# Half of a sparse weighted row sum taken from TensorE to VectorE, and the sparse work put in another order

## The chip, the cores and the metric

The kernel runs on one core of one Trainium2 chip. The metric is the device time of one execution in microseconds (us); lower is better. The median of three runs of the kernel before is 1426.06 us (1424.3 to 1428.26).

## The reference, cut to what matters

One layer on 512 tokens of width 1024, in float32. A token mixer and a LayerNorm come first, then PEER, a retrieval among 16384 experts, and a second LayerNorm. Only PEER matters for the change:

```
scores -> top 16 x 16 candidates -> expert_idx, gates     (8 heads x 16 = 128 experts per token)
u   = u_tab[expert_idx]                                   (128 rows of 1024 per token)
act = gelu(sum_d x[d] * u[k, d]) * gates[k]
out = sum_k act[k] * v_tab[expert_idx[k]]
x   = LayerNorm(alpha * x + out)
```

## The kernel before, in words

The kernel computes PEER in two ways at once. For the last 256 tokens it is dense: a main loop goes over the 128 blocks of 128 experts, loads a block of both tables (512 KB each) on SyncE's queue, and multiplies on TensorE, with the routing written out as a matrix `ring` that holds each token's gate for each expert. For the first 256 tokens, two groups of 128, it is sparse: GpSimd gathers single rows of the tables by indirect DMA, 128 rows (512 KB) to a gather, into nine buffers `gat` (`NGAT`, line 59).

**The sparse work.** It has two parts for each group i. The u part: gather j fetches, for each of the 128 tokens (one a partition), the row of its expert in slot j, by column j of `idxs[i]`. VectorE multiplies it with the token's x and sums up, which gives column j of `dots` (`sparse_u`, line 1042). When 128 columns are there, `sparse_act` makes `coef` of them (Gelu, times the gate), and `sparse_turn` transposes it on TensorE to `coefT`. The v part: gather t fetches all 128 experts' rows of one token, by column t of `idxT`, one expert a partition. `sparse_v` takes four such tiles, for the tokens r, 32 + r, 64 + r and 96 + r, and multiplies each on TensorE by a 128x32 piece of `expand`, a matrix of zeros with one column of coefficients, so that each token's sum lands in its own row of the two PSUM banks `facc` (line 1102). After 32 such groups the sums of 128 tokens are complete. `finish_a` then adds alpha times x from `x1s[i]`, and `finish_q`, `finish_s`, `finish_b` and `finish_c` make the LayerNorm.

**The order.** It is written out by hand. `gq` is the queue of gathers and `sparse` the queue of their consumers, in the same order; `pull` (line 1024) issues gathers while fewer than nine buffers are held. In the main loop, iteration b calls `work` four times, which takes consumers from the queue by a quota in units (`QUOTA`, line 63): 5 units an iteration up to iteration 13, 3.5 up to 30, then the rest of 512 spread evenly up to 125. A u counts 1 unit, a v group 4. The queue holds 128 u of group 0, then by turns 4 u of group 1 and one v group of group 0, then the finish of group 0, then the 32 v groups of group 1 and its finish.

**An iteration of the main loop** (line 1267) also has, for the dense part: `u_split` and `v_split`, which split a block into a high and a low part (ScalarE copies, VectorE subtracts, line 118); `h_run`, 24 matmuls for a block's activations (line 1261); `a_mul` and `a_low`, which scale them by the routing (lines 1004 and 118); and `v_tile`, 12 matmuls into PSUM (line 1253). Up to iteration 30 the matmuls with v are in plain float32 (line 1243). In three windows of iterations (`GWIN`, 14 to 30, 38 to 61, 70 to 93) VectorE also builds one-hot matrices (`g_hot`, lines 947 to 957), four instructions in two iterations of three, from which TensorE makes the next part of `ring`.

What must be free for what: each engine takes its instructions in program order. A gather waits for the buffer's last reader, on VectorE for a u and on TensorE for a v. The first v group of group 1 waits until `finish_a` has read the banks of group 0. The finish holds up to three of the nine buffers, for the rows of the norm and as scratch.

Of the kernel before, what the change touches and what calls it, by code (L numbers as in the profile page):

```python
# [10 lines left out]
F32 = mybir.dt.float32  # L11
# [3 lines left out]
I32 = mybir.dt.int32  # L15
U32 = mybir.dt.uint32
AF = mybir.ActivationFunctionType
OP = mybir.AluOpType
# [3 lines left out]
ALPHA = 2.0 ** 0.25  # L22
# [3 lines left out]
D = 1024  # L26
# [16 lines left out]
SPT = 256  # L43
# [58 lines left out]
def hybrid_kernel(ctx, tc, cst, xT, x, w_in, conv_a, vec_a, pool_w, conv_c, w_out, ln,  # L102
                  wq, keysT, uT, u, v, out):
    nc = tc.nc
    act, dve, pe, pool, sp = nc.scalar, nc.vector, nc.tensor, nc.gpsimd, nc.sync
# [8 lines left out]
    def copy_act(o, i, scale=1.0):  # L114
        return act.activation(o, i, AF.Copy, scale=scale)  # L115
# [29 lines left out]
    ident = const.tile([128, 128], F32, name="ident")  # L145
# [11 lines left out]
    x1s = [xtp.tile([128, D], F32, name=f"x1s{i}") for i in range(NU)]  # L157
# [7 lines left out]
    with ExitStack() as fctx:  # L165
# [31 lines left out]
        zero = mx.tile([128, T], BF, name="sp", bufs=1)  # L197
# [442 lines left out]
    mp = ctx.enter_context(tc.tile_pool(name="mp", bufs=1))  # L640
    ring = mp.tile([128, RB, ND], F32, name="ring")
    idxs = [mp.tile([128, 128], I32, name=f"idx{i}") for i in range(NU)]
    gss = [mp.tile([128, 128], F32, name=f"gs{i}") for i in range(NU)]
    idxT = mp.tile([128, SPT], I32, name="idxT")
    expand = mp.tile([128, 4, 31 + 32 * EH], F32, name="expand")
    usplit, uraw, gl = {}, {}, {}

# [42 lines left out]
    def ramp_fill(n):  # L690
        for _ in range(n):
            b, k = divmod(ramp[0], 8)
            if b == (ucount[1] if b < RSPL else RAMP):
                return
            if k == 0:
                ramp[1] = h_psum()
            if b < RSPL:
                h_part(b, ramp[1], [k])
                if k == 7:
                    ramp_split()  # L700
            else:
                u_load(b + 2)
                pe.matmul(ramp[1], uraw[b][:, k, :], native["x"][:, k, :], start=k == 0, stop=k == 7)  # L703
                if k == 7:
                    uraw.pop(b)
                    ucount[1] = b + 1
                    h_gelu(b, ramp[1])
            ramp[0] += 1
# [11 lines left out]
    with ExitStack() as rctx:  # L720
# [176 lines left out]
        def turn(src):  # L897
            ps = fps.tile([128, T], F32, name="b", bufs=6)
            for b in range(SPT // 128, NB):
                pe.transpose(ps[:, 128 * b:128 * b + 128], src[:, b, :], ident)  # L900
            return ps[:, SPT:]
# [12 lines left out]
        ef = rt.tile([128, NU, 128], F32, name="ef")  # L914
# [7 lines left out]
        copy_act(gTh, gf)  # L922
        copy_act(i2T, turn(i2v))
        eps_ = fps.tile([128, T], F32, name="b", bufs=6)
        for i in range(NU):
            pe.transpose(eps_[:, 128 * i:128 * i + 128], ef[:, i, :], ident)
            copy_act(gss[i], gm[:, i, :])
        sub(gTl, gf, gTh)
        ramp_fill(TFILL[3])
        dve.tensor_copy(idxT, eps_[:, :SPT])  # L930

    pctx.close()
    def g_hot(q, tg, where, bufs):
# [83 lines left out]
    gats, gq, sparse = {}, deque(), deque()  # L1017
    held = [0]


    def spare():
        return gp.tile([128, D], F32, name="gat", bufs=NGAT)

    def pull():
        while gq and held[0] < NGAT:
            kind, i, j = gq.popleft()
            t = spare()
            gats[kind, i, j] = t
            held[0] += 1
            if kind == "l":  # L1030
                sp.dma_start(t, ln[2 + i:3 + i, :].to_broadcast([128, D]))
            if kind == "x":
                sp.dma_start(t, x1d[:, NU + i, :])
            if kind not in "uv":
                continue
            table, idx = (u, idxs[i][:, j:j + 1]) if kind == "u" else (v, idxT[:, 128 * i + j:128 * i + j + 1])
            pool.indirect_dma_start(out=t, out_offset=None, in_=table,  # L1037
                                    in_offset=bass.IndirectOffsetOnAxis(ap=idx, axis=0))

    def sparse_u(i, j):  # L1040
        t = gats.pop(("u", i, j))
        dve.scalar_tensor_tensor(t, t, 1.0, x1s[i], op0=OP.mult, op1=OP.mult, accum_out=dots[:, j:j + 1])  # L1042
        held[0] -= 1

    def add_u(i, j):
        gq.append(("u", i, j))
        sparse.append((1, lambda: sparse_u(i, j)))
# [24 lines left out]
    mp2 = ctx.enter_context(tc.tile_pool(name="mp2", bufs=1))  # L1072
    coef = mp2.tile([128, 128], F32, name="coef")
# [4 lines left out]
    facc = [pacc.tile([128, 512], F32, name=f"facc{hf}") for hf in range(2)]  # L1078
# [14 lines left out]
    def sparse_expand(s):  # L1093
        o = 31 + 256 * (s % 2)
        copy_act(expand[:, :, o:o + 32 * 7 + 1:32], coefT[:, :, 8 * s:8 * s + 8])

    def sparse_v(i, r):
        ts = [gats.pop(("v", i, 32 * j + r)) for j in range(4)]
# [7 lines left out]
    fin = {}  # L1106

    def finish_a(key, f, x1):
        fs = mp2.tile([128, 4], F32, name="fs", bufs=4)
        sums, mean, sd = fs[:, 0:2], fs[:, 2:3], fs[:, 3:4]  # L1110
        for hf in range(2):
            cc = slice(512 * hf, 512 * hf + 512)
            dve.scalar_tensor_tensor(x1[:, cc], x1[:, cc], ALPHA, f[hf], op0=OP.mult, op1=OP.add,
                                     accum_out=sums[:, hf:hf + 1])
        dve.tensor_scalar(mean, sums[:, 0:1], sums[:, 1:2], -1.0 / D, op0=OP.add, op1=OP.mult)
        fin[key] = [x1, mean, sd, x1]

    def finish_q(key):
        x1, mean, sd = fin[key][:3]
        if ("s", key, 0) in gats:  # L1120
            junk = gats.pop(("s", key, 0))
            held[0] -= 1
        else:
            junk = spare()
        act.activation(junk, x1, AF.Square, bias=mean, accum_out=sd)
# [26 lines left out]
    def zero(f, *a):  # L1152
        sparse.append((0, lambda: f(*a)))

    def add_v(i, r):
        if r == 0:
            zero(sparse_expand, 1)
        if r in (9, 17):
            zero(sparse_expand, r // 8 + 1)
        for j in range(4):  # L1160
            gq.append(("v", i, 32 * j + r))
        sparse.append((4, lambda: sparse_v(i, r)))

    zero(sparse_act, 0)
    zero(sparse_clear)
    for k in range(34):
        if k < 32:
            for j in range(4):
                add_u(1, 4 * k + j)
        if k == 0:  # L1170
            zero(sparse_turn)
        if k == 1:
            zero(sparse_expand, 0)
        if k == 32:
            zero(sparse_act, 1)
        if k > 1:
            add_v(0, k - 2)
        if k == 32:
            zero(sparse_turn)
    gq.append(("s", 0, 0))  # L1180
    gq.extend(("l", i, 0) for i in range(2))
    zero(finish_a, 0, facc, x1s[0])
    zero(sparse_expand, 0)
    sparse.append((1, lambda: finish_q(0)))
    zero(finish_0)
    sparse.append((1, finish_1))
    for k in range(32):
        add_v(1, k)
    gq.extend(("l", i, 1) for i in range(2))
    gq.extend(("x", i, 0) for i in range(2))  # L1190
    sparse.append((1, lambda: finish_a(128, facc, x1s[1])))
    sparse.append((1, lambda: finish_q(128)))

    quota = []
    for end, n in QUOTA:
        i = end - len(quota)
# [170 lines left out]
```

## Time and profile before

| | |
|---|---|
| median of three runs | 1426.06 us |
| the profiled execution, its own time | 1420.93 us |
| its span | 1419.1 us |
| PE busy | 1322.5 us (93%) |
| DVE busy | 1086.8 us (77%) |
| POOL busy | 779.0 us (55%) |
| ACT busy | 512.5 us (36%) |
| moved by DMA | 439.83 MB, 310 GB/s in the mean |

PE is TensorE's matmuls, DVE VectorE, POOL GpSimd, ACT ScalarE. The shares of busy time are means over stages that differ: the first 410 us or so are the mixer and the routing, and the sparse work fills the rest. They are therefore read by stretches of the span. In a matmul's row the end is modelled, so rows of one line overlap. On VectorE too, an instruction's row can reach some 0.08 us into the next one's; what an instruction costs is the distance between two starts.

### The profile page before, as it was taken

The page shows a single profiled execution, that of the slowest core. Times are in us where ns is not written, and L with a number is a line of the kernel's source. Part 1 is how long each engine was busy: PE and PEld are TensorE (multiplying, and loading weights), DVE is VectorE, ACT ScalarE, POOL GpSimd, SP SyncE. Part 2 cuts the span into 40 slices and gives each one's busy share as a digit, 9 for nine tenths or more (in the row PEclk, how much of TensorE's full clock was granted, in tenths as well). Part 3 has the DMA queues.
Part 4 walks back from the last instruction along what each step waited for, and adds up shares of the span by engine and source line. Part 5 has one row for each costly group of instructions (what it writes and reads, how often), then busy time and mean ns, then how long its engine had stood idle before and what let it go on. Part 6 is the DMA issues. An engine that isn't in the chain of part 4 may idle for free.

```text
span 1419.1 us, 24250 instructions
## 1 busy us (share of the span) xinstructions
PE 1322.5 (93%) x9229; PEld 1006.2 (71%) x9229; DVE 1086.8 (77%) x2292; ACT 512.5 (36%) x735; POOL 779.0 (55%) x687
## 2 busy tenths in 40 slices
PE   9999999989995668998999999999999989999996
PEld 6787889989862234666677777777778767777774
DVE  7876669999987899998788888778888843444445
ACT  4654524321420001323344434334444443333333
POOL 2242317774537786667666665666656545455450
PEclk9999999999998888999999999999999999999998
DMA  6520323223659999999999999999999999999993
GB/s 212 186 63 13 134 84 128 83 75 110 229 199 389 420 411 367 378 375 375 413 377 392 388 385 390 405 419 404 405 403 402 406 364 416 402 419 409 419 408 141
DMA packets 125444, 439.83 MB, mean 310 GB/s; under 512 B 14480, under 2 KB 16528, under 8 KB 125328
## 3 DMA queue, kind: packets, MB, share of 16 engines
q0 software_dynamic: 73728, 268.47, 48.0%
q1 hardware_dynamic: 51312, 168.78, 31.6%
q8 instruction: 72, 1.18, 0.3%
q10 hardware_dynamic: 288, 1.05, 0.2%
q14 instruction: 44, 0.36, 0.1%
HBM read 435.09 MB, written 3.15 MB: 309 GB/s over the span
## 4 chain that ended last, share of the span: by engine, by line
PE 50%; issue 14%; DMA 13%; POOL 11%; DVE 10%; ACT 2%; POOLq 0%; DVEq 0%; SPq 0%; ACTq 0%
PE acc L1253 12%; PE w L1261 11%; POOL gat L1037 10%; DMA gat<-in_v,idxT 8%; PE facc L1102 8%; DMA gat<-in_u,idx 4%; PE b L138 4%; PE b L139 4%; PE b L137 4%; PE w L703 3%; DVE i_top L757 2%; DVE s_top L755 1%; PE z L312 1%; DVE sc L760 1%; DVE gat L1042 1%
## 5 line engine op out<-in xcount | busy, mean ns | idle before, releaser
L1037 POOL DMA_INDIRECT gat<-in_u,idx x256 | 336.5, 1314 | 222.5 <-DVE gat L1042 142.6
L1037 POOL DMA_INDIRECT gat<-in_v,idxT x256 | 280.6, 1096 | 178.6 <-PE facc L1102 100.1
L1042 DVE SCALAR_TENSOR_TENSOR gat<-gat,x1s 128x1024 f32<-128x1024 f32 x256 | 309.4, 1222 | 15.7 <-DMA gat<-in_u,idx 15.1
L1253 PE MATMUL acc<-vh,A 128*128 128x512 f32 x768 | 261.5, 401 | 0.0
L1261 PE MATMUL w<-x1Tdh,whi 128*128 128x256 f32 x832 | 241.7, 291 | 1.6 <-ACT gl L1264 1.4
L1261 PE MATMUL w<-x1Tdl,whi 128*128 128x256 f32 x832 | 235.2, 283 | 0.0
L1261 PE MATMUL w<-x1Tdh,wlo 128*128 128x256 f32 x832 | 234.9, 282 | 0.0
L118 DVE TENSOR_TENSOR vl<-vraw,vh 128x1024 fp32r<-128x1024 f32 x96 | 117.5, 1224 | 121.2 <-ACT vh L115 121.1
L1253 PEld LDWEIGHTS acc<-vh,A 128*128 128x128 f32 x768 | 145.1, 189 | 81.5 <-issue 28.5
L1243 PE MATMUL acc<-vraw,af 128*128 128x512 f32 x248 | 136.9, 697 | 48.6 <-DVE af L1004 45.2
L115 ACT ACTIVATE whi<-wraw 128x1024 fp32r<-128x1024 f32 (+1 forms) x146 | 151.0, 1036 | 48.6 <-DMA wraw<-in_wq 25.5
L1102 PE MATMUL facc<-gat,expand 128*32 128x512 f32 x1024 | 152.5, 600 | 14.8 <-DMA gat<-in_v,idxT 14.1
L1261 PEld LDWEIGHTS w<-x1Tdh,whi 128*128 128x128 f32 x832 | 159.4, 192 | 6.1 <-ACT gl L1264 2.3
L1261 PEld LDWEIGHTS w<-x1Tdl,whi 128*128 128x128 f32 x832 | 159.3, 191 | 2.4
L1261 PEld LDWEIGHTS w<-x1Tdh,wlo 128*128 128x128 f32 x832 | 159.0, 191 | 0.0
L118 DVE TENSOR_TENSOR wlo<-wraw,whi 128x1024 fp32r<-128x1024 f32 (+1 forms) x109 | 131.7, 1210 | 34.7 <-ACT whi L115 34.0
L115 ACT ACTIVATE vh<-vraw 128x1024 fp32r<-128x1024 f32 x96 | 101.4, 1056 | 143.5 <-issue 118.1
L1253 PE MATMUL acc<-vl,A 128*128 128x512 f32 x384 | 151.0, 393 | 0.0
L118 POOL TENSOR_TENSOR wlo<-wraw,whi 128x1024 fp32r<-128x1024 f32 x37 | 92.5, 2504 | 96.0 <-ACT whi L115 96.0
L1243 PEld LDWEIGHTS acc<-vraw,af 128*128 128x128 f32 x248 | 51.1, 219 | 112.3 <-DVE af L1004 61.2
L115 ACT ACTIVATE ring<-w 128x384 f32<-128x384 f32 (+2 forms) x80 | 52.4, 740 | 169.4 <-PE w L973 169.4
L1264 ACT ACTIVATE gl<-w 128x256 f32<-128x256 f32 x104 | 39.9, 384 | 185.3 <-PE w L1261 182.8
(301 smaller groups left out, 2376.8 us busy)
## 6 DMA issues: line engine op xcount, KB each, us to landing
wraw<-in_uT SPq DMA_DIRECT2D x128, 512.0 KB, 8.4
vraw<-in_v SPq DMA_DIRECT2D x128, 512.0 KB, 6.5
wraw<-in_w_in SPq DMA_DIRECT2D x18, 512.0 KB, 3.8
wraw<-in_wq SPq DMA_DIRECT2D x16, 512.0 KB, 3.9
wo<-in_w_out SPq DMA_DIRECT2D x8, 512.0 KB, 9.3
gat<-in_u,idx POOLq DMA_INDIRECT x256, 8.3
gat<-in_v,idxT POOLq DMA_INDIRECT x256, 6.9
wo<-in_xT SPq DMA_DIRECT2D x8, 256.0 KB, 5.5
```

The costliest lines, as they stand in the source:

```text
L115: return act.activation(o, i, AF.Copy, scale=scale)
L118: eng.tensor_tensor(out=o, in0=a, in1=b, op=OP.subtract)
L137: pe.matmul(ps, lh, rh, start=start, stop=False)
L138: pe.matmul(ps, lh, rl, start=False, stop=False)
L139: pe.matmul(ps, ll, rh, start=False, stop=stop)
L703: pe.matmul(ramp[1], uraw[b][:, k, :], native["x"][:, k, :], start=k == 0, stop=k == 7)
L1037: pool.indirect_dma_start(out=t, out_offset=None, in_=table, in_offset=bass.IndirectOffsetOnAxis(ap=idx, axis=0))
L1042: dve.scalar_tensor_tensor(t, t, 1.0, x1s[i], op0=OP.mult, op1=OP.mult, accum_out=dots[:, j:j + 1])
L1102: pe.matmul(facc[hf][32 * j:32 * j + 32, :], expand[:, j, o:o + 32], ts[j][:, 512 * hf:512 * hf + 512], start=r == 0, stop=r == 31)
L1243: pe.matmul(acc[hf], af[b][:, c:c + 128], raw[:, 512 * hf:512 * hf + 512], start=b == 0, stop=False)
L1253: pe.matmul(acc[hf], lhs[x], rhs[y], start=b == 0 and p == 0, stop=b == NI - 1 and p == 2)
L1261: pe.matmul(ps, w[:, k, :], x1Td[x][:, k, :], start=k == 0 and p == 0, stop=k == 7 and p == 2)
```

## The change

For group 1 (the second 128 tokens) the v part is no longer done on TensorE. Its gathers fetch by slot, as those of the u part do: gather j brings, for each of the 128 tokens, the row of v of its expert in slot j. VectorE multiplies the tile by column j of `coef`, a scalar for each partition, and adds it to `x1s[1]` in place (`sparse_f`). Before the first of these, ScalarE multiplies `x1s[1]` by alpha (`sparse_scale`). The last one also sums up each row, from which the mean follows, so `finish_a` is not called for group 1. `coef` of group 1 is not transposed. Group 0 stays as it was.

The order of the queues after the u of group 0 is now: 16 rounds of 8 u of group 1 and, from the second round, a v group of group 0; then 17 rounds of a v group of group 0 and six multiply-adds of group 1 (1 unit each); then the finish of group 0, with four multiply-adds between its steps; then the other 22 multiply-adds. `idxT` holds group 0 alone.

```diff
-    idxT = mp.tile([128, SPT], I32, name="idxT")
+    idxT = mp.tile([128, 128], I32, name="idxT")
...
-            if kind not in "uv":
+            if kind not in "uvf":
                 continue
-            table, idx = (u, idxs[i][:, j:j + 1]) if kind == "u" else (v, idxT[:, 128 * i + j:128 * i + j + 1])
+            table = u if kind == "u" else v
+            idx = idxT[:, j:j + 1] if kind == "v" else idxs[i][:, j:j + 1]
...
+    def sparse_scale():
+        copy_act(x1s[1], x1s[1], scale=ALPHA)
+
+    def sparse_f(j):
+        t = gats.pop(("f", 1, j))
+        more = {}
+        if j == 127:
+            fs = mp2.tile([128, 4], F32, name="fs", bufs=4)
+            more["accum_out"] = fs[:, 0:1]
+            fin[128] = [x1s[1], fs[:, 2:3], fs[:, 3:4], x1s[1]]
+        dve.scalar_tensor_tensor(x1s[1], t, coef[:, j:j + 1], x1s[1], op0=OP.mult, op1=OP.add, **more)
+        if j == 127:
+            dve.tensor_scalar(fs[:, 2:3], fs[:, 0:1], -1.0 / D, None, op0=OP.mult)
+        held[0] -= 1
...
+    def add_f(n):
+        for j in range(nf[0], nf[0] + n):
+            gq.append(("f", 1, j))
+            sparse.append((1, lambda j=j: sparse_f(j)))
+        nf[0] += n
+
+    nf = [0]
     zero(sparse_act, 0)
     zero(sparse_clear)
-    for k in range(34):
-        if k < 32:
-            for j in range(4):
-                add_u(1, 4 * k + j)
-        if k == 0:
-            zero(sparse_turn)
-        if k == 1:
-            zero(sparse_expand, 0)
-        if k == 32:
-            zero(sparse_act, 1)
-        if k > 1:
-            add_v(0, k - 2)
-        if k == 32:
-            zero(sparse_turn)
+    for k in range(16):
+        for j in range(8):
+            add_u(1, 8 * k + j)
+            if k == 0 and j == 0:
+                zero(sparse_turn)
+            if k == 0 and j == 4:
+                zero(sparse_expand, 0)
+        if k:
+            add_v(0, k - 1)
+    zero(sparse_act, 1)
+    zero(sparse_scale)
+    for r in range(15, 32):
+        add_v(0, r)
+        add_f(6)
     gq.append(("s", 0, 0))
     gq.extend(("l", i, 0) for i in range(2))
     zero(finish_a, 0, facc, x1s[0])
-    zero(sparse_expand, 0)
+    add_f(2)
     sparse.append((1, lambda: finish_q(0)))
     zero(finish_0)
+    add_f(2)
     sparse.append((1, finish_1))
-    for k in range(32):
-        add_v(1, k)
+    add_f(128 - nf[0])
     gq.extend(("l", i, 1) for i in range(2))
     gq.extend(("x", i, 0) for i in range(2))
-    sparse.append((1, lambda: finish_a(128, facc, x1s[1])))
     sparse.append((1, lambda: finish_q(128)))
```

## Rows read from the trace of the kernel before

**Rows 1.** By stretch: length, busy PE, PEld, DVE, ACT, POOL, clock, DMA share, GB/s.

```profile
460.00:505.00 45.00, 28.45 (x48) 10.89 (x48) 38.07 (x67) 0.00 (x0) 35.66 (x31) 0.85 1.03 419
515.00:638.00 123.00, 111.65 (x855) 70.75 (x856) 119.62 (x206) 29.55 (x50) 80.94 (x61) 0.94 0.99 377
638.00:697.00 59.00, 50.66 (x282) 36.30 (x281) 47.22 (x74) 19.81 (x32) 39.27 (x31) 0.97 1.00 390
697.00:890.40 193.40, 189.82 (x1564) 146.43 (x1562) 163.21 (x253) 82.64 (x113) 121.59 (x96) 1.00 1.00 388
890.40:944.00 53.60, 50.71 (x307) 38.70 (x304) 36.94 (x55) 19.81 (x29) 34.19 (x30) 1.00 1.02 411
944.00:1013.50 69.50, 68.39 (x577) 54.55 (x576) 63.10 (x99) 29.78 (x46) 43.72 (x35) 1.00 1.02 411
1013.50:1126.00 112.50, 111.30 (x922) 88.09 (x916) 98.07 (x154) 47.72 (x74) 69.59 (x57) 1.00 1.01 402
1126.00:1178.00 52.00, 47.23 (x338) 33.56 (x341) 23.94 (x35) 23.04 (x37) 26.27 (x24) 1.00 0.97 378
1178.00:1339.00 161.00, 161.00 (x1096) 117.68 (x1092) 69.48 (x84) 59.13 (x87) 82.54 (x84) 1.00 1.02 412
1339.00:1393.00 54.00, 54.00 (x372) 39.33 (x368) 23.16 (x28) 19.94 (x29) 22.26 (x23) 1.00 1.01 399
```

**Rows 2.** The same stretches, line 1004 on DVE alone: once an iteration.

```profile
460.00:505.00 45.00, 2.55 (x6) 0.85 1.03 419
515.00:638.00 123.00, 6.93 (x17) 0.94 0.99 377
638.00:697.00 59.00, 2.94 (x7) 0.97 1.00 390
697.00:890.40 193.40, 10.08 (x24) 1.00 1.00 388
890.40:944.00 53.60, 2.92 (x7) 1.00 1.02 411
944.00:1013.50 69.50, 3.77 (x9) 1.00 1.02 411
1013.50:1126.00 112.50, 5.87 (x14) 1.00 1.01 402
1126.00:1178.00 52.00, 2.53 (x6) 1.00 0.97 378
1178.00:1339.00 161.00, 8.92 (x21) 1.00 1.02 412
1339.00:1393.00 54.00, 2.98 (x7) 1.00 1.01 399
```

**Rows 3.** The chain of waits in 697 to 890 us, shares by line.

```profile
by line: DMA gat<-in_v,idxT 19.2%; POOL gat L1037 17.6%; PE acc L1253 17.2%; issue 16.4%; PE w L1261 15.5%; PE facc L1102 10.0%; PE w L972 2.2%; PE w L973 2.2%; POOLq L1037 0.2%
```

**Rows 4.** The v groups on TensorE, from the page's costliest groups.

```profile
L1102 PE MATMUL facc<-gat,expand 128*32 128x512 f32 x1024 | 152.5, 600 | 14.8 <-DMA gat<-in_v,idxT 14.1
```

**Rows 5.** Two u products in order of time on DVE: start, length.

```profile
579.18 1.21 DVE L1042 SCALAR_TENSOR_TENSOR gat<-gat,x1s 128x1024 f32<-128x1024 f32 x1
...
580.32 1.21 DVE L1042 SCALAR_TENSOR_TENSOR gat<-gat,x1s 128x1024 f32<-128x1024 f32 x1
```

**Rows 6.** Near the end, DVE in order of time: start, length.

```profile
1411.38 1.28 DVE L1134 SCALAR_TENSOR_TENSOR gat<-gat,fs 128x1024 f32<-128x1024 f32 x1
1412.58 0.16 DVE L1138 RECIPROCAL fs<-fs 128x1 f32<-128x1 f32 x1
```

**Rows 7.** Lines 389 and 1042 on DVE: busy us, mean ns, idle before; ns min/median/max.

```profile
L389 DVE SCALAR_TENSOR_TENSOR hA<-ua,cva,hA 128x512 f32<-128x512 f32 x30 | 28.6, 954 | 0.0
L389 DVE SCALAR_TENSOR_TENSOR hA<-ua,cva,hA x30: 734/740/2886, 22.6 to 106.2; 128x512 f32<-128x512 f32 x30
L1042 DVE SCALAR_TENSOR_TENSOR gat<-gat,x1s 128x1024 f32<-128x1024 f32 x256 | 309.4, 1222 | 15.7 <-DMA gat<-in_u,idx 15.1 <-DVE gat L1042 0.4
L1042 DVE SCALAR_TENSOR_TENSOR gat<-gat,x1s x256: 1208/1217/1294, 411.5 to 1122.7; 128x1024 f32<-128x1024 f32 x128
```

More of the change, by code (lines that the diff above doesn't have):

```diff
@@ L924, in hybrid_kernel @@
         eps_ = fps.tile([128, T], F32, name="b", bufs=6)
+        pe.transpose(eps_[:, :128], ef[:, 0, :], ident)
         for i in range(NU):
-            pe.transpose(eps_[:, 128 * i:128 * i + 128], ef[:, i, :], ident)
             copy_act(gss[i], gm[:, i, :])
@@ L929, in hybrid_kernel @@
         ramp_fill(TFILL[3])
-        dve.tensor_copy(idxT, eps_[:, :SPT])
+        dve.tensor_copy(idxT, eps_[:, :128])
     pctx.close()
```

## The prediction, made before the changed kernel was built or run

> **What bounds the kernel now.** I read four views in this order. First the busy table by stretch, cut at the iterations of the main loop from 460 us on; the reader is to see that DMA moves 377 to 419 GB/s in all of it while no engine is full in all of it [rows 1]. Then the count of one DVE instruction that occurs once an iteration (line 1004), in the same stretches: length over count is the time of an iteration [rows 2]. Then the chain of waits in the stretch 697 to 890, and last single DVE instructions.
>
> Iterations, from rows 1 and 2: with gathers for u only, 45.0/6 = 7.50 us at 419 GB/s; I take this as what the transfers allow, because DVE (38.07 of 45.0), PE (28.45) and POOL (35.66) all have room there. From 515 to 638, DVE is busy 119.62 of 123.0, or 97.3%: that is how full DVE gets. In the mixed stretches, where four u and a group of four v alternate, 59.0/7 = 8.43, 193.4/24 = 8.06, 53.6/7 = 7.66, 69.5/9 = 7.72 and 112.5/14 = 8.04. Where group 0 is finished, 52.0/6 = 8.67. With v only, 161.0/21 = 7.67, PE busy 161.00 of 161.00, at 412 GB/s, so PE and the transfers are nearly level. Transfers per iteration are the same everywhere: 412 x 161.0/21 = 3.16 MB, 419 x 45.0/6 = 3.14 MB.
>
> In the mixed stretch the chain runs 19.2% through v gathers in flight, 17.6% through POOL issuing, and 42.7% through three PE lines [rows 3]: supply of rows and PE take turns. That is what a group of four produces: it waits for its last row and then frees four buffers together.
>
> **The change part by part.** *What leaves.* 32 groups of `sparse_v` for the second 128 tokens, half of line 1102: 152.5/64 = 2.38 us a group by the profile's modelled ends [rows 4], so up to 76 us of PE. Also one transpose of `coef`, two `expand` copies, and half of the `idxT` work, all once and small. The gathers leave too, and as many come back with the same bytes.
>
> *What comes.* 128 multiply-adds of 128x1024 on DVE. No such instruction is in the trace. The nearest from below is the u product, whose starts lie 1.14 us apart (579.18 to 580.32) [rows 5]. The nearest in form, two SBUF tensors and a scalar from a column, is line 1134: 1.28 long, the next starts 1.20 later [rows 6]. From above, the convolution's multiply-add in place: 0.734 at its shortest but 0.954 in the mean for half the elements, so 1.9 for all of them [rows 7]. I take 1.20, the row with the same shape and operands, and keep 1.14 and 1.9 as ends. Together 128 x 1.20 = 154 us of DVE for at most 76 of PE.
>
> *What moves.* Counted from the code: from iteration 31 a quota of (512 - 129)/95 = 4.03 units an iteration. Before, u and v alternate 4 to 4 until iteration 94, then v. After, 8 u to 4 v until 77 (188 units), then 4 v to 6 of the new kind until 120 (170 units), then the new kind alone. SP's loads for the finish of group 0 move from iteration 94 to 120, behind as many loads of blocks as before; POOL's queue holds the same number of gathers, in order of use. The new wait: a multiply-add that waits for its row holds DVE's queue, that is the splits and `a_low` behind it, and `v_tile` on PE behind those. The u products wait so now, 15.1 us in 256 [rows 7], in stretches with the same transfers, so I count nothing for it.
>
> Now by stretch. DVE per iteration now is its busy time over the count [rows 1, 2]. In 31 to 77 there are 4.03 x (8/12 - 4/8) = 0.67 more u, which at 1.14 is 0.77 us.
> - 638 to 697: the start of mixing. Same start, so -1 (from +1 to -6.5, if it reached 7.50).
> - 697 to 890: DVE 163.21/24 = 6.80, after 7.57; at 97.3% that is 7.78. The other end is 8.06 as now. Middle, 7.92: 24 x -0.14 = -3.4 (-6.7 to the rival below).
> - 890 to 944: DVE 36.94/7 + 0.77 = 6.05, not the bound; the transfers leave 7.66 to 7.50. 0 (-1.2 to 0).
> - 944 to 1013: DVE 63.10/9 + 0.77 = 7.78, at 97.3% 8.00 against 7.72: 9 x 0.28 = +2.5.
> - 1013 to 1126: DVE 98.07/14 = 7.00; the 2.03 u (2.3 us) give way to 4.03 x 0.6 x 1.20 = 2.9 us: 7.60, at 97.3% 7.81; the middle to 8.04 is 7.92: 14 x -0.12 = -1.6 (-3.2 to the rival below).
> - 1126 to 1178: PE, DVE and the chain no longer meet at the hand-over of the two PSUM banks from group 0 to group 1; what is late next is PE at 7.67. 6 x (7.67 - 8.67) = -6.0.
> - 1178 to 1339: 0.4 groups an iteration on PE in place of 1, DVE 69.48/21 + 2.9 = 6.2. The bound is the transfers, 7.50; the middle to 7.67: 21 x -0.09 = -1.9 (-3.6 to 0).
> - 1339 to 1393, 7 iterations: 27 multiply-adds, 32.4 us; the finish of group 0, which is the DVE surplus of 1126 to 1178, 23.94 - 6 x 3.31 = 4.1; and 7 times the present 23.16/7 = 3.31, which in packed sequence (starts 1.14 apart for 1.21 long) is about 3.0, so 21. Sum 57.5, at 97.3% 59.1 against 54.0: +5.1. DVE is the bound here, with three of nine buffers held by the finish.
> - After the loop: two multiply-adds (2.4) stand where `finish_a` had two halves, by the same row about one full width (1.2) [rows 6]: +1.
>
> The sum is -1 - 3.4 + 0 + 2.5 - 1.6 - 6.0 - 1.9 + 5.1 + 1 = -5.3. The profiled execution took 1420.93 us (span 1419.1), so 1415.6; the median of the runs shown is 1426.06, 5.1 higher, so **1420.8** in its terms.
>
> The added cost of PE's idling is nothing only while the granted clock stays at 1.00; it is so from 697 to 1393, and it was 0.85 at 460 to 505, where PE was busy 63% [rows 1]. The last seven iterations come near that; a slower PE would hide behind DVE.
>
> **A rule weighed.** Line 1042 never took over 1.294 us in 256 instances, while POOL issued gathers all along; line 389, whose last start at 106.2 lies before the gathers, reached 2.886 with 0.740 in the median [rows 7]. So gathers did not hold such an instruction, whatever held line 389, and I keep 1.20. The Trainium skill (SBUF — State Buffer, "Who interferes with whom") says that a DVE instruction with two SBUF inputs contends with a GpSimd one that reads SBUF. By that rule the new multiply-adds, which have two SBUF inputs, would stretch wherever gathers read their index; for gathers the trace disagrees, and the result it would give is rival 4.
>
> **Rivals.**
> 1. *DVE becomes the bound, and its idle stays.* Each iteration of 697 to 890 has 8.06 - 6.80 = 1.26 us of DVE idle, partly round trips through ScalarE. If none of it can be filled, the added work comes on top: +0.77 x 24 = 18.5, 0.77 x 9 = 6.9, 0.60 x 14 = 8.4, +7 in the last seven iterations, +1, less 6.0: +36, 1462. At half of the idle it is about +8, 1434. It decides from some 0.5 us kept an iteration. For it: 93% or more of each iteration would be DVE. Against it: the 97.3% of 515 to 638.
> 2. *Supply improves throughout.* Single buffers come free one at a time, iterations fall to 7.50 or DVE's 97.3%: -6.5 - 6.7 - 1.2 + 2.5 - 3.2 - 7 - 3.6 + 3.5 (57.5 against 54.0) + 1 = -21, 1405. For it: the u stretch at 419 GB/s. Against: 890 to 944 mixes at little DVE load and is no better than 7.66.
> 3. *No change.* Where PE is taken off, the transfers hold the iteration at 7.67, and the hand-over's 6 us come back in the last seven iterations: 1426. For it: 412 against 419 GB/s leaves 1.7%. Against: the hand-over is a wait on PE's banks, which goes.
> 4. *The multiply-add is held by POOL* and takes 1.9: +0.7 x 128 = 90 us of DVE, about half of it exposed, +45 with the forecast's -5, 1466. For it: line 389. Against: line 1042.
>
> **How the numbers follow.** The forecast's case has 0.38, rival 1 0.25, rival 2 0.16, rival 3 0.18, rival 4 0.03. Within 0.3% (4.3 us) is about what a measurement can tell from no change. The forecast at -5.3 is close to that line and I give it 0.32 beyond it and 0.06 inside. So faster 0.32 + 0.16 = 0.48, same 0.18 + 0.06 = 0.24, slower 0.28. The forecast's own range is 1412 to 1428; the range of all is 1402 to 1446, which leaves out the full rivals 1 and 4 and the far end of 2.
>
> **What would show it.** The multiply-add's starts 1.20 apart; iterations of 697 to 890 near 7.9 with DVE at 95% or more; no 8.67 at the hand-over; 7.5 to 7.67 with 412 GB/s or more in the v and multiply-add stretch; DVE full in the last seven iterations at about 8.4 us. It is wrong if the mixed iterations go above 8.3 (rival 1), if they fall to 7.6 (rival 2), or if the multiply-add takes over 1.3.

## The result and the profile after

The changed kernel is slower: 1435.07 us in the median of nine runs (1430.93 to 1444.85) against 1427.00 for the kernel before (nine runs, 1422.08 to 1431.41), a ratio of 1.0068 [1.0049, 1.0087], in brackets the 95% interval. That is +8.1 us where -5.3 was forecast. The profiled execution took 1434.59 us, near its median; the one of before took 1420.93, 6 us below its own. A comparison of the two traces therefore shows 13.7 us, of which about 5.6 are the choice of executions.

The page of the kernel after, its span, its busy time, and three groups (busy us, mean ns of one, idle before):

```profile
span 1432.8 us, 23454 instructions
PE 1294.4 (90%) x8715; PEld 997.9 (70%) x8715; DVE 1230.3 (86%) x2417; ACT 508.5 (35%) x731; POOL 841.4 (59%) x687
L1043 DVE SCALAR_TENSOR_TENSOR gat<-gat,x1s 128x1024 f32<-128x1024 f32 x256 | 308.9, 1223 | 16.3 <-DMA gat<-in_u,idx 15.1
L1108 DVE SCALAR_TENSOR_TENSOR x1s<-gat,coef,x1s 128x1024 f32<-128x1024 f32 x128 | 163.9, 1280 | 0.9
L1118 PE MATMUL facc<-gat,expand 128*32 128x512 f32 x512 | 121.5, 638 | 36.6 <-DMA gat<-in_v,idxT 36.3
```

L1108 is the new multiply-add, L1118 the v groups of group 0 (L1102 before, [rows 4]), L1043 the u product (L1042 before, [rows 7]). Of the v groups half the matmuls have gone, but their busy time fell by 31 us and not by 76: the mean of one rose from 600 to 638 ns, and the idle time ahead of them from 14.8 to 36.6 us.

The busy table by stretch, cut as for [rows 1] at the starts of line 1004 in the same iterations (31, 38, 62, 69, 78, 92, 98, 119, 126); columns as there:

```profile
639.80:697.60 57.80, 49.76 (x272) 37.24 (x273) 51.25 (x82) 19.64 (x32) 36.97 (x28) 0.92 0.98 376
697.60:893.70 196.10, 186.88 (x1500) 145.32 (x1495) 180.41 (x285) 82.09 (x112) 134.84 (x97) 1.00 1.00 385
893.70:950.00 56.30, 52.36 (x297) 38.93 (x298) 41.22 (x63) 19.45 (x29) 35.32 (x29) 0.97 1.01 403
950.00:1023.10 73.10, 69.16 (x554) 53.78 (x556) 67.67 (x109) 29.59 (x48) 47.58 (x37) 1.00 1.01 389
1023.10:1139.90 116.80, 111.93 (x926) 91.66 (x919) 105.23 (x130) 48.08 (x76) 69.33 (x56) 0.97 0.99 384
1139.90:1187.90 48.00, 43.59 (x276) 30.94 (x275) 36.61 (x40) 18.55 (x28) 32.07 (x26) 0.96 1.00 393
1187.90:1351.50 163.60, 152.75 (x892) 114.38 (x891) 126.12 (x134) 58.19 (x85) 98.77 (x82) 0.99 1.02 404
1351.50:1408.40 56.90, 46.40 (x270) 39.59 (x269) 56.44 (x64) 22.41 (x33) 35.87 (x25) 0.94 1.00 390
```

Set beside [rows 1] and the forecast's sum (us; iterations counted as in [rows 2]):

| iterations | before | after | after - before | forecast |
|---|---|---|---|---|
| start to 30 | | | +1.4 | none |
| 31-37 | 58.9 | 57.9 | -1.0 | -1 |
| 38-61 | 193.3 | 196.1 | +2.8 | -3.4 |
| 62-68 | 53.5 | 56.2 | +2.7 | 0 |
| 69-77 | 69.5 | 73.2 | +3.7 | +2.5 |
| 78-91 | 112.5 | 116.7 | +4.2 | -1.6 |
| 92-97 (hand-over of the banks) | 52.2 | 48.0 | -4.2 | -6.0 |
| 98-118 | 161.0 | 163.6 | +2.6 | -1.9 |
| 119-125 | 53.7 | 56.9 | +3.2 | +5.1 |
| after the loop | 26.1 | 24.3 | -1.8 | +1 |

The gain at the hand-over is there. What is missing is spread over the stretches in which u, v and multiply-adds mix, 38 to 91 and 98 to 118, which came out 1.2 to 6.2 us worse than forecast and in which the transfers move 384 to 404 GB/s where before they moved 388 to 412. So the reader should look for who waits for rows. The view of waits has the idle time of TensorE ahead of the v groups (us in total, times, longest). It has two rows for the same waits, one for the weight loads (PEld) and one for the matmuls (PE), which must not be added up. Before, 64 groups:

```profile
PEld facc L1102 <- DMA gat<-in_v,idxT: 38.8, 36, 3.7
PE facc L1102 <- DMA gat<-in_v,idxT: 14.1, 16, 2.8
```

and after, 32 groups:

```profile
PEld facc L1118 <- DMA gat<-in_v,idxT: 83.0, 56, 2.5
PE facc L1118 <- DMA gat<-in_v,idxT: 36.3, 44, 1.6
```

By the weight loads that is 0.61 us a group before and 2.59 after, by the matmuls 0.22 and 1.13: four to five times as long. A load can wait while earlier matmuls still run, and a matmul's modelled end reaches into a wait, so the time lost lies between the two: 22 to 44 us more of waiting stand against the 76 us that the prediction allowed for the groups removed. (The 53 and 119 us that expectations below name are the sums of both rows.) In order of time on TensorE (start, length, idle before), one such group:

```profile
767.72 1.99 PE L1118 MATMUL facc<-gat,expand 128*32 128x512 f32 x6
771.25 1.90 PE L1118 MATMUL facc<-gat,expand 128*32 128x512 f32 x10 [1.53 <-DMA gat<-in_v,idxT]
```

Its first rows were there and its last was not. The chain of waits in 697.6 to 893.7, shares by line, says the same: against [rows 3] the v rows in flight rose from 19.2 to 29.0%, POOL's issuing from 17.6 to 33.7%, and TensorE's three largest lines, 42.7% before, have given way to two with 7.5%.

```profile
by line: POOL gat L1038 33.7%; DMA gat<-in_v,idxT 29.0%; issue 22.8%; DMA gat<-in_u,idx 4.7%; PE facc L1118 4.6%; PE acc L1275 2.9%; DVE vl L118 0.6%; DVE ohB L957 0.6%; ACT vh L115 0.5%; POOLq L1038 0.3%; DVE ohAg L954 0.2%; DVE ohA L947 0
```

In iterations 69 to 77 it is another thing. The busy table, one row for each of the first six iterations, cut at the starts of line 1004:

```profile
950.06:959.96 9.90, 9.90 (x66) 9.05 (x65) 9.87 (x19) 2.82 (x4) 6.65 (x5) 1.00 1.02 381
959.96:968.76 8.80, 7.11 (x47) 3.35 (x46) 8.77 (x17) 2.58 (x4) 3.93 (x4) 1.00 1.01 403
968.76:974.66 5.90, 5.90 (x66) 5.35 (x65) 4.37 (x8) 3.71 (x6) 4.68 (x5) 1.00 1.01 362
974.66:984.46 9.80, 9.80 (x76) 8.78 (x75) 9.77 (x17) 3.83 (x6) 6.56 (x5) 1.00 1.03 412
984.46:993.26 8.80, 7.95 (x54) 4.30 (x53) 8.77 (x17) 2.59 (x4) 5.53 (x5) 1.00 0.99 385
993.26:998.96 5.70, 5.70 (x64) 5.19 (x64) 4.40 (x8) 3.69 (x6) 4.79 (x4) 1.00 0.98 365
```

By these cuts the first two of three iterations hold four and three u products and a one-hot build each, and VectorE is full (9.87 of 9.90, 8.77 of 8.80); the third holds one u product and no build, and there TensorE is full (5.90 of 5.90) and VectorE at 74%. TensorE is full in the first as well (9.90 of 9.90) and idles in the second, where the v group waits for its rows. Over the nine iterations VectorE is busy 67.67 of 73.10, 93%: the sum leaves 5.4 us free, but nearly all of it lies in the third iterations, where VectorE waits for work and TensorE is full or nearly so.

### The profile page after: what moved, and what is told of

It reads as the page before. It is cut to its first block, busy times and chain, and to the rows that moved or that the text cites. A ratio compares the mean times of both kernels' runs of the same rounds, so it can differ in the third digit from the quotient of the medians.

```text
span 1432.8 us, 23454 instructions
## 1 busy us (share of the span) xinstructions
PE 1294.4 (90%) x8715; PEld 997.9 (70%) x8715; DVE 1230.3 (86%) x2417; ACT 508.5 (35%) x731; POOL 841.4 (59%) x687
## 3 DMA queue, kind: packets, MB, share of 16 engines
q8 instruction: 68, 1.11, 0.3%
## 4 chain that ended last, share of the span: by engine, by line
PE 26%; issue 19%; DVE 19%; DMA 18%; POOL 15%; ACT 2%; POOLq 0%; DVEq 0%; SPq 0%; ACTq 0%
POOL gat L1038 15%; DMA gat<-in_v,idxT 13%; DMA gat<-in_u,idx 4%; PE b L138 4%; PE b L139 4%; PE b L137 4%; DVE gat L1043 4%; PE facc L1118 3%; DVE x1s L1108 3%; PE w L703 3%; PE acc L1275 3%; PE w L1283 2%; DVE ohB L957 2%; DVE i_top L757 1%; DVE s_top L755 1%
## 5 line engine op out<-in xcount | busy, mean ns | idle before, releaser
L1038 POOL DMA_INDIRECT gat<-in_u,idx x256 | 344.3, 1345 | 172.4 <-issue 57.2
L1043 DVE SCALAR_TENSOR_TENSOR gat<-gat,x1s 128x1024 f32<-128x1024 f32 x256 | 308.9, 1223 | 16.3 <-DMA gat<-in_u,idx 15.1
L1283 PE MATMUL w<-x1Tdh,whi 128*128 128x256 f32 x832 | 244.8, 294 | 5.1 <-ACT gl L1286 4.8
L1038 POOL DMA_INDIRECT gat<-in_v,idx x128 | 171.8, 1342 | 103.2 <-DVE x1s L1108 48.3
L1038 POOL DMA_INDIRECT gat<-in_v,idxT x128 | 163.8, 1280 | 80.7 <-DVE x1s L1108 26.4
L1275 PEld LDWEIGHTS acc<-vh,A 128*128 128x128 f32 x768 | 146.2, 191 | 58.9 <-issue 18.7
L1108 DVE SCALAR_TENSOR_TENSOR x1s<-gat,coef,x1s 128x1024 f32<-128x1024 f32 x128 | 163.9, 1280 | 0.9
L1118 PE MATMUL facc<-gat,expand 128*32 128x512 f32 x512 | 121.5, 638 | 36.6 <-DMA gat<-in_v,idxT 36.3
L115 ACT ACTIVATE A<-af 128x256 fp32r<-128x256 f32 x97 | 40.6, 418 | 260.8 <-DVE af L1004 260.8
```

The costliest lines, as they stand in the source:

```text
L1038: pool.indirect_dma_start(out=t, out_offset=None, in_=table, in_offset=bass.IndirectOffsetOnAxis(ap=idx, axis=0))
L1108: dve.scalar_tensor_tensor(x1s[1], t, coef[:, j:j + 1], x1s[1], op0=OP.mult, op1=OP.add, **more)
L1118: pe.matmul(facc[hf][32 * j:32 * j + 32, :], expand[:, j, o:o + 32], ts[j][:, 512 * hf:512 * hf + 512], start=r == 0, stop=r == 31)
L1275: pe.matmul(acc[hf], lhs[x], rhs[y], start=b == 0 and p == 0, stop=b == NI - 1 and p == 2)
L1283: pe.matmul(ps, w[:, k, :], x1Td[x][:, k, :], start=k == 0 and p == 0, stop=k == 7 and p == 2)
```

## The experiments

The runs come in three groups, the first and the third on one chip, the second on another; the kernel before took 1424.9, 1432.0 and 1433.7 us in them. So ratios to the kernel before in the same group are compared, and an expected time is to be set beside 1427.0 times the ratio. Stretches are read from one profile of each run. The same code gave 194.0, 196.1, 200.4 and 200.9 us in iterations 38 to 61 in four profiles (`e1_order_alone`, the kernel after, `hot_after`, `e3_thin`), so a difference of under 5 us in that stretch is no evidence by itself.

**Rows issued earlier, in the kernel after.** The buffers get names and a free list, and the four gathers of a v group are issued ahead of up to four u, or three multiply-add, gathers that stood before them.

```diff
+    def ahead_of(order, steps):
+        ...
+            while n < run and n < steps.get(out[-1][0], 0) and out[-1 - n][0] == out[-1][0]:
+                n += 1
+            run = 0
+            out[len(out) - n:len(out) - n] = four
+        order.extend(out)
+
+    ahead_of(gq, {"u": 4, "f": 3})
```

> The changed kernel with one thing different: the four gathers of a v group are issued ahead of the four u (or three multiply-adds) that come before the group, while the consumers keep their order and the buffers stay nine. Supply theory (in the changed order the last row of a v group is issued only about one iteration before TensorE needs it, behind the u or multiply-adds whose buffers it has to wait for; TensorE's waits for v rows grew from 53 us in 64 groups to 119 us in 32): the waits fall to 60 us or less, iterations 38 to 77 come back from about 8.1 to 8.0 us or less and 98 to 118 from 7.79 to 7.65, time 1423 to 1428. Rival, DVE is the bound (its added 154 us are what costs): DVE's work is the same, so the time stays at 1435 within 3 us.

Measured: 1447.01 us, ratio 1.0130 [1.0102, 1.0158]; slower still, which neither theory expected. In its profile, of the slowest of seven executions (1456.24 us), the v groups' wait fell from 83.0 to 36.6 us by the weight loads and from 36.3 to 19.8 by the matmuls, as it should, but VectorE now waited. In the view of waits (us in total, times, longest):

```profile
DVE gat L1051 <- DMA gat<-in_u,idx: 46.1, 35, 7.8
DVE x1s L1117 <- DMA gat<-in_v,idx: 43.9, 17, 6.0
```

In the kernel after the first was 15.1 us in 21 waits, and the second, a multiply-add waiting for its row, did not occur. What was taken from one consumer was given to the other: as far as these views show, with nine buffers the order of issue chooses who waits. The theory that rows issued too late were the fault fell here.

**The same in the kernel before**, ahead of two u: `ahead_of(gq, {"u": 2, "f": 0})`.

> The kernel before with the same edit alone: the four gathers of a v group are issued ahead of the two u that come before it. Supply theory: there the row of a v group was late by less (0.8 us a group), so at most half of 53 us of waits goes, and part of it is hidden: -2 to -6 us, 1421 to 1425. Rival, DVE is the bound: no change, within 2 us of 1427.

Measured: 1423.74 us, 0.9982 [0.9957, 1.0007]: inconclusive. In its profile iterations 38 to 61 took 189.6 us, 3.7 less than before, and 69 to 77 took 77.0, 7.5 more.

**The new order alone.** All of the v part of group 1 on TensorE again, in the order 8 u to 4 v (against the kernel after, cut to the order).

```diff
     for r in range(15, 32):
         add_v(0, r)
-        add_f(6)
+    zero(sparse_turn)
...
-    add_f(128 - nf[0])
+    for k in range(32):
+        add_v(1, k)
```

> The new order of u and v (8 u to 4 v) alone, with the v part of the second 128 tokens still on TensorE as 32 groups. Supply theory: iterations 38 to 77 as in the changed kernel (about 8.17, 8.03 and 8.13 us by stretch), so +8 us there; from 78 to 93 v groups in every iteration beside the one-hot matmuls make TensorE the bound, near 8.5, another +7; the hand-over from group 0 to group 1 stays: 1440 to 1445. Rival, the multiply-adds are what costs: the order by itself is harmless, 1427 within 4 us.

Measured: 1440.36 us, 1.0087 [1.0057, 1.0117]. The order alone comes out as slow as the whole change, though about half of its loss is of another kind. The busy table of its iterations 62-68, 69-77, 78-91 and 92-97:

```profile
892.51:950.44 57.93, 53.11 (x298) 38.80 (x291) 41.17 (x65) 19.45 (x29) 36.01 (x30) 0.97 1.00 391
950.44:1023.84 73.40, 68.53 (x558) 53.78 (x560) 67.77 (x110) 29.46 (x47) 47.27 (x36) 1.00 0.99 384
1023.84:1142.86 119.02, 119.02 (x1024) 87.92 (x1020) 67.69 (x98) 48.54 (x75) 65.43 (x56) 1.00 1.00 377
1142.86:1198.92 56.06, 51.34 (x361) 35.95 (x357) 23.74 (x34) 23.51 (x36) 26.55 (x24) 0.97 0.95 362
```

Up to iteration 77 the code is that of the kernel after, and so is the loss in 62 to 77 (57.93 and 73.40 against 56.30 and 73.10). By its profile the iterations 38 to 77 take 9.1 us more than before (0.8, 4.4 and 3.9; the first is within the spread of that stretch). The 10.3 us more of 78 to 97 are another loss and split nothing: here TensorE is full, 119.02 of 119.02, because a v group falls in every iteration, and the hand-over is worse than before.

**The multiply-adds alone**, in the old order of 4 u to 4 v, and behind the v of group 0.

```diff
-    for k in range(16):
-        for j in range(8):
-            add_u(1, 8 * k + j)
...
+    for k in range(34):
+        if k < 32:
+            for j in range(4):
+                add_u(1, 4 * k + j)
...
+        if k > 1:
+            add_v(0, k - 2)
```

> The multiply-adds alone, in the old order: 4 u to 4 v until iteration 93 as before, then the finish of group 0 and 128 multiply-adds with no v group beside them. Supply theory: up to iteration 92 nothing changes (8.05, 7.65, 7.72 and 8.04 us an iteration), the hand-over loses some 4 us, and from there DVE bounds at about 8.0 in place of 7.67, +9: 1429 to 1434. Rival, DVE's 154 us are what costs wherever they stand: 1435 or more.

Measured: 1427.52 us, 1.0010 [0.9990, 1.0031]: no difference from before that can be told (1428.4 by the ratio, where 1429 to 1434 was expected). Iterations 38 to 91 are as before (192.4, 53.0, 71.0, 112.7 us). From 98 on VectorE is full, and those iterations lose 3.9 and 1.3 us, while 92 to 97 win 2.2 (92-97, 98-118 and 119-125 below):

```profile
1131.92:1181.96 50.04, 45.82 (x313) 37.80 (x313) 37.56 (x47) 23.30 (x35) 28.76 (x23) 0.93 0.97 377
1181.96:1346.90 164.94, 138.44 (x766) 114.92 (x764) 164.19 (x170) 54.23 (x84) 123.58 (x85) 0.94 1.02 404
1346.90:1401.85 54.95, 44.69 (x248) 37.35 (x249) 54.70 (x58) 18.07 (x28) 36.49 (x25) 0.94 1.00 388
```

**A tenth buffer.** In the main loop at most two of the three staging tiles of `load_raw` hold a block that is still to be split; the third becomes the tenth gather buffer, with the names and the free list of the runs above and the issue order unchanged. This does a second thing: with two tiles the load of a block has to wait until VectorE has split an earlier one. SyncE's queue shows it in the view of waits (us in total, times, longest), in the kernel after and with the tenth buffer:

```profile
SPq L126 <- DVE wlo L118: 2.4, 1, 2.4
SPq L129 <- DVE wlo L118: 315.8, 62, 8.7
```

No run has two staging tiles and nine gather buffers, so what the buffer does and what the later loads do is not separated in the runs below. First in the kernel after:

```diff
+        if n == NGAT:
+            return wts.tile([128, 8, 128], F32, name=f"wraw{tenth[0]}", bufs=1).rearrange("p a c -> p (a c)")
...
-        while gq and held[0] < NGAT:
+        while gq and held[0] < NGAT + len(tenth):
...
+    tenth.append(cycle.popleft())
+    free.append(NGAT)
```

> The changed kernel with a tenth gather buffer in the main loop (the third of the staging buffers for blocks of u, which then alternate in two). After the runs in which the rows were issued earlier, the supply theory reads: the rate of gathers is set by nine buffers over the time that each is held (wait for POOL, some 8 us in flight, wait for the consumer), whatever the order of issue; the new order holds them longer. Expected: one buffer more gives up to a ninth where supply is the bound, so iterations 38 to 118 fall from 8.2, 8.0, 8.1, 8.3 and 7.8 to 7.6 to 7.9, and the time from 1435 to 1415 to 1425. Rival, DVE is the bound: no change within 3 us of 1435. Second rival, the transfers themselves are at their limit: no change either, with the same GB/s.

Measured: 1425.10 us, 0.9951 [0.9933, 0.9968]: the edit turns the loss into a gain on the kernel before. Iterations 38-61, 62-68, 69-77 and 78-91:

```profile
699.74:889.80 190.06, 182.37 (x1506) 145.51 (x1505) 179.90 (x287) 80.72 (x112) 126.16 (x96) 1.00 1.01 397
889.80:941.84 52.04, 49.14 (x288) 37.92 (x287) 41.28 (x64) 19.23 (x29) 38.91 (x31) 1.00 1.03 419
941.84:1015.72 73.88, 68.26 (x561) 53.70 (x559) 67.71 (x108) 29.48 (x48) 47.62 (x36) 1.00 1.01 397
1015.72:1133.67 117.95, 110.12 (x911) 90.34 (x910) 105.07 (x130) 47.34 (x76) 72.65 (x56) 0.97 0.99 381
```

The first two fall by 6.0 and 4.2 us, to 7.92 and 7.43 an iteration, below all four profiles of this order with nine buffers; the last two don't fall (73.1 and 116.8 in the kernel after). So there are two limits, and the one of 38 to 68 gives way to this edit; that the buffer does it, and not the later loads, is argued. The chain in the first stretch has the v rows in flight at 4.1% where it was 29.0%:

```profile
by line: POOL gat L1051 44.0%; issue 42.4%; DMA gat<-in_u,idx 5.1%; DMA gat<-in_v,idxT 4.1%; POOL wraw L1051 3.2%; PE facc L1136 1.0%; POOLq L1051 0.5%; PE acc L1316 0.5%; another core or an unknown queue 0.0%
```

The same edit in the kernel before:

> The kernel before with the same tenth buffer. Supply theory: less is to be had, as there TensorE waits only 53 us for v rows and 28 iterations at the end are bound by TensorE: iterations 38 to 92 from 8.0 to about 7.7, the hand-over from 8.7 to 8.0, so 1408 to 1418. Rival, the transfers are at their limit: no change within 3 us of 1426.

Measured: 1419.55 us, 0.9915 [0.9892, 0.9937]. And in the kernel of the multiply-adds alone:

> The multiply-adds in the old order, with the tenth buffer. Supply theory: as the kernel before with ten buffers up to iteration 92; from there DVE at 7.85 an iteration stays the bound, so 1412 to 1422, and not below the kernel before with ten buffers. Rival, the transfers are at their limit: 1427 within 3 us.

Measured: 1422.12 us, 0.9937 [0.9919, 0.9955]. The edit is worth 0.0085 to the kernel before, 0.0073 to the old order with multiply-adds, and 0.0117 to the kernel after (1.0068 less 0.9951): by the medians most where eight u stand between two v groups, though the intervals don't part this from the kernel before. The times are as expected, one stretch is not: in the old order iterations 38 to 61 grew, from 193.3 to 198.9 us in the kernel before and from 192.4 to 197.5 with multiply-adds. Nine buffers were not the limit of that stretch there; the gain lies in others (in the kernel before 58.9 to 55.2 in 31-37, 53.5 to 51.3 in 62-68, 52.2 to 49.9 in 92-97). And by the medians the change stays behind the kernel before with the same edit.

**Thin multiply-adds.** 127 of the 128 work on 8 columns of 1024.

```diff
-        dve.scalar_tensor_tensor(x1s[1], t, coef[:, j:j + 1], x1s[1], ...)
+        n = D if j == 127 else 8
+        dve.scalar_tensor_tensor(x1s[1][:, :n], t[:, :n], coef[:, j:j + 1], x1s[1][:, :n], ...)
```

> The changed kernel with 127 of the 128 multiply-adds on 8 of 1024 columns (the other 1016 columns of the sum are left out): some 135 us of DVE work gone, gathers and order the same. Supply theory: nothing changes up to iteration 77 (8.17, 8.03, 8.13 us); after that buffers of the multiply-adds come free sooner, 78 to 91 from 8.34 to about 8.0, 98 to 118 from 7.79 to 7.6, the last seven from 8.13 to 7.6: 1422 to 1427. Rival, DVE's multiply-adds are the whole cost: 1415 or less. With either, iterations 38 to 77 show the part that the multiply-adds cannot explain.

Measured: 1420.41 us, 0.9898 [0.9872, 0.9923]. By the ratio that is 1412, below the 1422 to 1427 of the supply theory and within the rival's 1415 or less. Up to iteration 77 it is the kernel after, and as slow (200.9, 59.2 and 74.0 us in 38-61, 62-68 and 69-77). Then 78-91, 98-118 and 119-125:

```profile
1034.47:1140.03 105.56, 104.05 (x879) 85.35 (x880) 71.96 (x131) 48.90 (x76) 64.96 (x56) 1.00 1.02 410
...
1189.89:1346.25 156.36, 144.97 (x880) 111.53 (x879) 76.87 (x134) 58.57 (x84) 86.91 (x79) 1.00 1.02 416
1346.25:1394.20 47.95, 44.81 (x278) 39.94 (x277) 30.61 (x64) 23.00 (x33) 30.91 (x25) 0.96 1.03 418
```

Against the kernel after, the width of the multiply-add costs 11.2, 7.2 and 9.0 us there, 27 in all; the two ratios, 1.0068 and 0.9898, lie 0.017 apart, or 24 us. That is three times the net loss of the change. Against the kernel before, these profiles have the thin kernel 17.8 us longer in 38 to 77 and 19.7 shorter in 78 to 125: what the order costs in the first, the groups taken from TensorE would win in the second, and the full width of the multiply-adds takes that away again. It also shows what the transfers allow when VectorE is free: 7.45 and 6.85 us an iteration.

**The one-hot builds moved.** In the kernel after, the 16 builds of the third window go to iterations that have not four u or four multiply-adds, as far as there are any.

```diff
-            plan.setdefault(lo + (hi - lo) * tg // NG, []).append((q, tg))
+            at = {3: [70, 71, 73, 74, 76, 77, 78, 80, 82, 83, 85, 87, 88, 90, 92, 93]}.get(q)
+            plan.setdefault(at[tg] + 1 if at else lo + (hi - lo) * tg // NG, []).append((q, tg))
```

> The changed kernel with the 16 one-hot builds of the third window put at iterations that have neither four u nor four multiply-adds (70, 71, 73, 74, 76 to 78, 80, 82, 83, 85, 87, 88, 90, 92, 93). Balance theory (from 69 to 92 DVE bounds single iterations of four u or four multiply-adds with a one-hot build, 9.8 to 10 us, and what the light iterations leave cannot be saved up for them): iterations 69 to 77 go from 8.13 to about 7.9 and 78 to 91 from 8.34 to about 8.1, so 5 us less, ratio to the kernel before 1.003 in place of 1.007. Rival, the sum of DVE's work over several iterations counts, or supply alone: no change, ratio 1.006 to 1.008.

Measured: 1437.33 us, 1.0034 [1.0011, 1.0057]; the interval overlaps that of the kernel after, so by itself this run settles nothing. By its profile iterations 69-77 took 74.71 us, no better, and 78-91 109.54, 7.2 less, while 38-61 (200.4) and 98-118 (166.1) took more. With the tenth buffer as well:

> The changed kernel with the tenth buffer and the one-hot builds of the third window moved. If supply bounds 38 to 68 and balance 69 to 92, the two gains add up: the tenth buffer's ratio 0.995 to the kernel before goes to about 0.991. If balance is no cause, 0.995 stays.

Measured: 1414.29 us, 0.9881 [0.9852, 0.9911], below the 0.9951 of the buffer alone, with the intervals apart. Iterations 69-77 and 78-91, against 73.88 and 117.95 there:

```profile
934.25:1005.84 71.59, 69.03 (x531) 54.13 (x529) 67.52 (x109) 29.31 (x46) 48.28 (x36) 0.98 1.02 409
1005.84:1113.78 107.94, 104.97 (x891) 86.47 (x892) 100.38 (x123) 47.22 (x76) 75.50 (x56) 1.00 1.02 407
```

In 78-91 VectorE has 4.7 us less to do (100.38 against 105.07, as the last builds lie past the cut), and the stretch is 10.0 us shorter: where the work lay counted, beside how much there was. (The one-hot matmuls on TensorE move with their builds, so which engine's balance counted is not separated.) Last, the kernel before with the tenth buffer and the builds of its second window moved to iterations with one u, as far as possible:

```diff
+            at = {2: [38, 40, 42, 43, 44, 46, 48, 49, 50, 52, 54, 55, 56, 58, 60, 61], }.get(q)
```

> The kernel before with the tenth buffer, and with the 16 one-hot builds of the second window put mostly at iterations of one u (the even ones, and 43, 49, 55, 61). Balance theory: iterations 38 to 61, where three u, a v group and a one-hot build now meet in eight iterations, fall by 0.1 to 0.3 us each, so the ratio to the kernel before goes from the 0.9915 of ten buffers alone to about 0.988. Rival: no change, 0.9915.

Measured: 1416.11 us, 0.9877 [0.9850, 0.9903]; 38-61 fell from 198.86 (with the buffer alone) to 190.5 us. With the tenth buffer and one window's builds moved, the kernels with and without the change are equal (0.9881 and 0.9877), and both beat the two kernels of this case.

## Why the prediction was wrong

**The step that failed** is the one sentence on supply: "POOL's queue holds the same number of gathers, in order of use". The sum has no term for the time that a buffer is held, nor for TensorE's waits for v rows: each mixed stretch was put between the present iteration and 97.3% of VectorE, and none above the present unless VectorE's sum was. (The wait that it did set at nothing, a multiply-add's for its row, came out so.) The number of gathers is the same; who holds the buffers is not. Worked out from the rows of 38 to 61, from the issue of a gather to the end of the instruction that reads the buffer, a u buffer was held 17.9 us in the mean before and a v buffer 13.0; after, 17.1 and 13.7. With eight u to four v more of the gathers are of the longer kind, 65 of 97 in place of 48 of 95, and the mean of all goes from 15.5 to 16.0 us, with nine buffers. A slower iteration also lengthens the holding, so this describes the loss and does not prove its cause; that the order costs time is shown by the runs at 1.0087 and 1.0010. TensorE's wait grew from 0.22 to 1.13 us a group by the matmuls (0.61 to 2.59 by the loads). The tenth buffer brings iterations 38 to 61 to 7.92, the very value forecast for nine, with the block loads later as well; in the old order it only lengthened the holding of a u buffer, from 17.9 to 21.1 us. 38 to 68 came out 8.9 us above the forecast, more than the whole gain that was forecast. The four profiles with this order and nine buffers have 194.0 to 200.9 us in 38-61 and 56.0 to 59.2 in 62-68; the two with the old order have 192.4 and 193.3, and 53.0 and 53.5.

**The second failed step** is the measure. I added up VectorE's work over a stretch and divided by its iterations (7.78 for 69-77, 7.60 for 78-91). But in 69 to 74 a heavy iteration lasts as long as VectorE needs, up to 9.9 us, and a light one as long as TensorE needs, 5.7 to 5.9. What is lost in the one isn't won back in the other. For 78 to 91 that is the likely part of what made -1.6 into +4.2: the moved builds bring it to 109.54, with the tenth buffer to 107.94, and so below the forecast's 110.9 (112.5 - 1.6). The +2.5 for 69 to 77 was right in sign and measured +3.7.

**98 to 125.** I held the transfers to be the bound at 7.50, by a stretch that moved 419 GB/s. `e3_thin` went to 7.45 and 6.85, and the kernel before with ten buffers to 7.33 in 62-68, so 7.50 was no limit. With full multiply-adds 98-118 takes 7.79 with VectorE busy only 77%, and the chain there goes through v rows in flight 31.4%, POOL's issuing 21.3%; the tenth buffer changes it little (162.09). That their width costs 7 us is shown, by which wait is not. In 119 to 125 VectorE is full, 56.44 of 56.90, as forecast, and the size was off by 1.9 (+3.2, not +5.1).

**What held.** The multiply-add on VectorE (start, length), and the next start 1.20 later, as taken from [rows 6]:

```profile
1380.09 1.28 DVE L1108 SCALAR_TENSOR_TENSOR x1s<-gat,coef,x1s 128x1024 f32<-128x1024 f32 x1
1381.29 1.22 DVE L118 TENSOR_TENSOR vl<-vraw,vh 128x1024 fp32r<-128x1024 f32 x1
```

All 128 lie between 1272 and 1324 ns, so rival 4 (held by POOL) is out. The hand-over gave 4.2 of the 6.0 us. No multiply-add waited for its row. The fallen clock of the last iterations (0.94, TensorE busy 46.40 of 56.90) did hide behind VectorE.

**The rivals.** Rival 2 and 3 are out. Rival 1, VectorE's idle that can't be filled, had 1434 for half of it, next to the 1435.07 measured, which is partly luck, and its turning point of 0.5 us an iteration was passed: (196.10 - 180.41)/24 = 0.65 in 38 to 61. But its reason was half right. In 69 to 91 VectorE is full in single iterations; in 38 to 68 its idle is kept, by the chain of waits, mostly because rows come late, to TensorE above all.

**The rule weighed.** I asked whether gathers hold a VectorE instruction, and they don't. The trace shows the other direction, on POOL (start, length, idle before) and on VectorE in the same microseconds:

```profile
760.23 1.68 POOL L1038 DMA_INDIRECT gat<-in_v,idxT  x1 [0.61 <-DVE gat L1043]
762.51 1.68 POOL L1038 DMA_INDIRECT gat<-in_v,idxT  x1 [0.60 <-DVE gat L1043]
```

```profile
759.88 1.22 DVE L118 TENSOR_TENSOR vl<-vraw,vh 128x1024 fp32r<-128x1024 f32 x1
761.02 1.22 DVE L1043 SCALAR_TENSOR_TENSOR gat<-gat,x1s 128x1024 f32<-128x1024 f32 x1
...
762.16 1.22 DVE L1043 SCALAR_TENSOR_TENSOR gat<-gat,x1s 128x1024 f32<-128x1024 f32 x1
...
763.30 0.42 DVE L1004 SCALAR_TENSOR_TENSOR af<-gl,ring 128x256 f32<-128x256 f32 x1
```

The 59 gathers of this trace that start while VectorE is idle take 0.93 to 0.95 us. These two took 1.68, and less 0.94 they were held until 760.97 and 763.25, when the VectorE instruction then running gave way to the next (761.02, 763.30). Of the 173 gathers that start with 0.3 to 0.9 us of a VectorE instruction of 1024 columns left, all took 1.11 us or more. In the mean the issue of a v row of group 0 went from 1.19 to 1.28 us. The Trainium skill (SBUF — State Buffer, "Who interferes with whom") says that issue order decides which of the two blocks, and the same page's "Summary: rules for kernel authors" that the second to issue then stands until the first has finished. For the gathers the trace agrees; for VectorE behind a gather it shows no such stand (1272 to 1324 ns). How much of the loss this is was not separated: it lengthens the time for which a buffer is held, as a fuller VectorE does, and in the kernel at 1.0010 the gathers for the multiply-adds took 1.45 us in the mean.

## What to carry to other kernels

Before an order of prefetched work is changed, divide the number of buffers by the time for which each is held, from issue to release: that is the rate that they allow, and a count of transfers that stays the same says nothing of it. Add up an engine's work iteration by iteration and take the largest engine in each, since light iterations don't pay back heavy ones. And time an order and an operation apart: here the operation on another engine, in the old order, cost nothing net that can be measured (1.0010), the new order by itself did (1.0087, about half of it by v groups that the change doesn't have), and a tenth buffer in the kernel before, with its later block loads (0.9915), was worth more than any of it.

## Not expected of the hardware

In the kernel after the issue of a gather on POOL took 0.93 us at its shortest and up to 2.02 us, and the two long ones shown above end 0.89 us after a VectorE instruction of two inputs has given way to the next. One core's transfers reached 418 to 419 GB/s, and 6.85 us an iteration where VectorE was free, against the 7.50 that looked like their limit.
